# The last two output products of a decoder layer: one order of rows for both column halves, weights split on chip, the residual put into the accumulator banks, and the normalisation on one engine

## The chip, the cores and the metric

One core of a Trainium2 chip. The metric is the device time of one execution in microseconds, the median of several runs; three runs of the kernel before gave 1638.19, 1639.03 and 1640.66. Times in the traces are counted in microseconds from the start of the span of one profiled execution. The engines are TensorE (PE in the profile; PEld is its weight load), VectorE (DVE), ScalarE (ACT), GpSimd (POOL) and SyncE (SP), whose queue issues all the DMAs spoken of here.

## The reference, cut to what matters

```python
# x: 1024 x 2048 float32; proj = x @ w_in, then attention, short convolution and pooling give y
y = jnp.concatenate([y_att, y_conv, y_pool], axis=-1)        # 1024 x 2048
y = jnp.einsum('bse,ed->bsd', y, w_out[l])                   # 2048 x 2048 weights
x = layer_norm(DEEPNORM_ALPHA * x + y, ln_g[l], ln_b[l])     # alpha = 2 ** 0.25

def layer_norm(x, g, b):
    mu = jnp.mean(x32, axis=-1, keepdims=True)
    var = jnp.mean(jnp.square(x32 - mu), axis=-1, keepdims=True)
    return (x32 - mu) * lax.rsqrt(var + LN_EPS) * g + b
```

## The kernel before

Both large products are computed by a scheme of seven half-size products in place of eight. Each float32 operand is split into a high and a low part (`split`, lines 120 to 122: ScalarE casts the high part, VectorE subtracts to get the low one), and each product of two 128-row blocks is three matmuls into one accumulator bank (`mm3`, lines 127 to 130: high x high, high x low, low x high). A bank is 128 x 512 float32; there are eight, four tagged `acc` and four tagged `aux`.

The change is in the output projection. Its seven products are named y11, ys3, ys2, ys1, y22, y12 and ys4, each done for the two column halves i = 0 and 1 of the result, in that order (`sequence`). `out_product` takes one product for one half: for each of eight blocks k it fetches a split weight block (`next_w`, from a running plan of loads) and multiplies it with four row tiles st, into four banks. At the last k the banks are emptied by `evac`. The result has four quarters of rows and columns per half: c11, c12 (rows 0 to 511) and c21, c22 (rows 512 to 1023). y22 completes c21, y12 completes c11, ys4 completes c12; c22 is complete before. `preset_at` puts alpha * x into a bank before the product starts, on ScalarE (line 1065), so that matmuls add to it; the finished bank is added to the tile in SBUF on VectorE (line 1092), and `stats_of` takes the statistics of that piece (line 1024).

Side work (loads, splits, presets, normalisation) is put into slots by `at` and taken out by `tick` after every third triple of matmuls; a scheduler then sets the order on each engine. Loads of weights and of y share four buffers tagged `wr`, so a load waits until the split of the block four loads back is done; stores of the result stand on the same SP queue.

The last product, ys4 for i = 1, is written by hand. Its eight weight blocks are kept whole (`keep_w`: load, then split into `wlast`), and it goes row by row: row tile st takes all eight k into one bank, the bank is added to c12 (line 1227), its statistics are taken, and the row is normalised at once. The last row is done in two half-width parts, so it has two banks of 256 columns.

`norm_steps` normalises one row tile of 128 rows. `stats` combines the statistics and does five small instructions and a square root on ScalarE (line 1128). Each of four pieces of 512 columns then takes a first step (subtract the mean, multiply with g, line 1150) and a second step (multiply with the inverse deviation, add b, line 1151), both on VectorE, and is stored (line 1152). In the tail, that is for the rows 0 to 3 which come last, two of four pieces (one in the last row) go another way:

```python
if tail and c in ((1, 2) if s < 3 else (2,)):
    nc.scalar.activation(r, r, AF.Identity, bias=nt[:, 3:4], scale=nt[:, 2:3])
    nc.gpsimd.tensor_tensor(r, r, g, ALU.mult)
    nc.gpsimd.tensor_tensor(r, r, b, ALU.add)
```

That is one instruction on ScalarE (line 1146) and two on GpSimd (lines 1147 and 1148). Rows 4 to 7 (c21, c22) are normalised earlier, beside y12, on VectorE alone.

Of the kernel before, what the change touches and what calls it, by code (L numbers as in the profile page):

```python
# [36 lines left out]
ALU = mybir.AluOpType  # L37
# [36 lines left out]
def layer(ctx: ExitStack, tc: tile.TileContext, xt, x, wp, wf, b_f, conv_w, pool_w, pool_scale,  # L74
# [903 lines left out]
    for name in WEIGHTS:  # L978
        for i in range(2):
            if (name, i) != ("ys4", 1):  # L980
                plan.extend(WEIGHTS[name](i, k) for k in range(KH))
# [68 lines left out]
    out_banks, last_x = {}, [None]  # L1050

    def preset_at(slot, name, i, st, tag):
# [67 lines left out]
    def norm_steps(s, tail=False):  # L1120
        env = {}

        def stats():
# [10 lines left out]
            if tail:  # L1134
                nc.vector.tensor_scalar(nt[:, 3:4], mv[:, 0:1], nt[:, 2:3], -1.0, ALU.mult, ALU.mult)
            env["mv"], env["nt"] = mv, nt

        def piece(c):
            def go():
# [15 lines left out]
        return [stats] + [piece(c) for c in ((2, 1, 0, 3) if tail else range(4))]  # L1155

    last = {}

    def keep_w(k, slot):
        def load():  # L1160
            last[k] = half("wl", "wr")
            nc.sync.dma_start(last[k], WEIGHTS["ys4"](1, k))

        def parts():
            t = hl("wlast", "xb")
            split_tile(t, last[k])
            last[k] = t

        at(slot, load)
        at(slot + 2, parts)  # L1170

    def after(name, i):
# [20 lines left out]
        if name == "y22":  # L1193
# [4 lines left out]
            else:  # L1198
# [3 lines left out]
                for k in range(KH):  # L1202
                    keep_w(k, 2 + 5 * k // 2)
# [3 lines left out]
    for n, (name, i) in enumerate(sequence[:-1]):  # L1207
        out_product(name, i, tag_of(n))
        after(name, i)
        if n + 2 < len(sequence) and (sequence[n + 2] == ("ys2", 1) or sequence[n + 2][0] in GOES_TO):  # L1210
            for st in range(4):
                preset_at(2 + st, *sequence[n + 2], st, tag_of(n + 2))
    for st in range(4):
        cuts = [0, H] if st < 3 else [0, H // 2, H]
        sl = slice(st * P, st * P + P)
        for n, (c0, c1) in enumerate(zip(cuts, cuts[1:])):
            acc = out_banks["ys4", 1, st]
            if n:
                acc = bank("acc")
                nc.scalar.activation(acc[:, c0:], last_x[0][:, c0:], AF.Copy, scale=ALPHA)  # L1220
            for k in range(KH):
                yt, w = xs["ys4", k], last[k]
                mm3(acc[:, c0:c1], yt[:, 0, sl], yt[:, 1, sl], w[:, 0, c0:c1], w[:, 1, c0:c1], False, k == KH - 1,
                    skip_group_check=True)
# [4 lines left out]
        while side:  # L1229
            for step in side.popleft():  # L1230
                step()
        for step in norm_steps(st, True):
            step()
# [43 lines left out]
```

## Time and profile before

| | |
|---|---|
| median of three runs | 1639.03 us (1638.19 to 1640.66) |
| the profiled execution | 1636.92 us, its span 1635.2 us |
| TensorE | 1553.2 us busy, 6836 instructions |
| VectorE | 1132.4 us busy, 1651 instructions |
| ScalarE | 702.0 us busy, 1254 instructions |
| GpSimd | 400.0 us busy, 317 instructions |
| DMA | 339.92 MB, mean 208 GB/s |

The span runs from the first to the last recorded event of the profiled execution; 1.7 us lie around it. Busy time counts an engine's instructions without its waits. Matmuls overlap, so the start of one and of the next tell more than their durations. In a timeline row, "x4" merges neighbours of the same kind, and the bracket gives the idle time just before and what ended it.

### The profile page before, as it was taken

How to read it: one execution, taken by the hardware profiler on the slowest of the kernel's cores; microseconds unless marked ns; L12 is line 12 of the kernel's file. 1: busy time of each engine (PE TensorE's matmuls, PEld its weight loads, DVE VectorE, ACT ScalarE, POOL GpSimd, SP SyncE). 2: the span in 40 equal slices, each digit the busy share in tenths (PEclk: the TensorE clock that was granted, in tenths of full speed). 3: DMA queues.
4: the chain of work that ended last, by engine and by line, in shares of the span. 5: the costliest groups of instructions: out<-in, count | busy, mean ns of one | idle time of the engine just before them, and what ended most of it. 6: DMA issues, size and time to landing. Idle time of an engine off the chain costs nothing. (4 is left out here: it accounts for less than half of the span.)

```text
span 1635.2 us, 20207 instructions
## 1 busy us (share of the span) xinstructions
PE 1553.2 (95%) x6836; PEld 1254.1 (77%) x6836; DVE 1132.4 (69%) x1651; ACT 702.0 (43%) x1254; POOL 400.0 (24%) x317
## 2 busy tenths in 40 slices
PE   8999999999999999999999999999988998999985
PEld 6887878877788777788877777868776776888765
DVE  6754666666666656478787868586779874567878
ACT  4421221112112225566665656575666554344431
POOL 0132232222222220012222323252326231100005
PEclk9999999999999999999999999999999999999998
DMA  8756988887878667534545454536344437557552
GB/s 248 261 206 208 323 286 291 302 293 257 301 254 306 237 241 247 216 133 160 181 159 177 149 193 149 181 116 210 124 166 142 160 118 251 174 186 231 183 191 103
DMA packets 156807, 339.92 MB, mean 208 GB/s; under 512 B 17952, under 2 KB 27040, under 8 KB 156704
## 3 DMA queue, kind: packets, MB, share of 16 engines
q1 hardware_dynamic: 156704, 338.64, 60.6%
q8 instruction: 53, 0.87, 0.2%
q14 instruction: 50, 0.41, 0.1%
HBM read 247.28 MB, written 91.29 MB: 207 GB/s over the span
## 5 line engine op out<-in xcount | busy, mean ns | idle before, releaser
L122 DVE TENSOR_TENSOR wh<-wr,wh 128x512 fp32r<-128x512 f32 x272 | 204.0, 755 | 97.7 <-ACT wh L121 97.3
L121 ACT CAST wop<-wb 128x1024 fp32r<-128x1024 f32 x76 | 80.0, 1053 | 322.9 <-PE acc L129 142.5
L121 ACT CAST wh<-wr 128x512 fp32r<-128x512 f32 x272 | 166.4, 618 | 94.2 <-DMA wr<-w_out 29.1
L128 PE MATMUL acc<-x,wh 128*128 128x512 f32 x448 | 178.7, 399 | 2.1 <-ACT wh L121 2.1
L130 PE MATMUL aux<-xs,wop 128*128 128x512 f32 x448 | 175.5, 392 | 5.4 <-DVE wop L122 5.2
L130 PE MATMUL acc<-x,wh 128*128 128x512 f32 x448 | 178.3, 398 | 2.3 <-DVE wh L122 2.2
L129 PE MATMUL acc<-x,wh 128*128 128x512 f32 x448 | 176.8, 395 | 0.0
L128 PE MATMUL aux<-xs,wop 128*128 128x512 f32 x448 | 174.6, 390 | 0.0
L129 PE MATMUL aux<-xs,wop 128*128 128x512 f32 x448 | 174.4, 389 | 0.0
L122 DVE TENSOR_TENSOR wop<-wb,wop 128x1024 fp32r<-128x1024 f32 x76 | 107.0, 1408 | 28.2 <-ACT wop L121 28.1
L130 PEld LDWEIGHTS acc<-x,wh 128*128 128x128 f32 x448 | 85.2, 190 | 27.0 <-DVE wh L122 8.9
L130 PEld LDWEIGHTS aux<-xs,wop 128*128 128x128 f32 x448 | 84.1, 188 | 27.3 <-DVE wop L122 9.6
L128 PEld LDWEIGHTS acc<-x,wh 128*128 128x128 f32 x448 | 85.1, 190 | 21.0 <-ACT wh L121 5.4
L129 PEld LDWEIGHTS aux<-xs,wop 128*128 128x128 f32 x448 | 84.1, 188 | 17.6
L128 PEld LDWEIGHTS aux<-xs,wop 128*128 128x128 f32 x448 | 84.1, 188 | 17.4
L129 PEld LDWEIGHTS acc<-x,wh 128*128 128x128 f32 x448 | 85.2, 190 | 15.7
L130 PE MATMUL acc<-xs,wh 128*128 128x512 f32 x224 | 87.7, 392 | 3.0 <-DVE wh L122 3.0
L130 PE MATMUL acc<-xs,wop 128*128 128x512 f32 x224 | 88.0, 393 | 2.7 <-DVE wop L122 2.5
L122 DVE TENSOR_TENSOR pt<-t,pt 128x512 fp32r<-128x512 f32 (+1 forms) x96 | 84.5, 894 | 6.5 <-ACT pt L121 6.3
L128 PE MATMUL acc<-xs,wh 128*128 128x512 f32 x224 | 88.3, 394 | 0.0
L129 PE MATMUL acc<-xs,wh 128*128 128x512 f32 x224 | 87.3, 390 | 0.0
L128 PE MATMUL acc<-xs,wop 128*128 128x512 f32 x224 | 87.2, 389 | 0.0
(266 smaller groups left out, 3628.3 us busy)
## 6 DMA issues: line engine op xcount, KB each, us to landing
wb<-wp SPq DMA_DIRECT2D x116, 512.0 KB, 5.6
wr<-wp SPq DMA_DIRECT2D x112, 256.0 KB, 2.9
wo<-w_out SPq DMA_DIRECT2D x64, 256.0 KB, 5.9
o_dram<-wo SPq DMA_DIRECT2D x64, 256.0 KB, 4.6
wr<-o_dram SPq DMA_DIRECT2D x64, 256.0 KB, 2.9
t_dram<-wb SPq DMA_DIRECT2D x28, 512.0 KB, 6.2
a_dram<-ca SPq DMA_DIRECT2D x28, 512.0 KB, 3.8
b_dram<-cb SPq DMA_DIRECT2D x28, 512.0 KB, 4.7
```

What stands on the lines that cost most here:

```text
L121: nc.scalar.copy(hi, src)
L122: nc.vector.tensor_tensor(lo, src, hi.bitcast(F32), ALU.subtract)
L128: nc.tensor.matmul(acc, wh, xh, start=start, stop=False, **more)
L129: nc.tensor.matmul(acc, wh, xl, start=False, stop=False, **more)
L130: nc.tensor.matmul(acc, wl, xh, start=False, stop=stop, **more)
```

## The change

The last two products, ys4 for both halves, are now both written by hand (`last_product`), and all sixteen weight blocks are loaded and split outside the running plan (`load_last`, `split_last`). The right half's blocks go where they went; the left half's go into the buffers of y12, and their loads are placed beside the first of the four parts below. The order is: rows 0 and 1 of the right half, rows 0 and 1 of the left half, then row 2 of both halves, then row 3 of both halves. The last row is no longer cut in two.

The preset of a ys4 bank is now alpha * x + c12 in one VectorE instruction. So the finished bank holds the finished piece: it isn't added to c12, its statistics are taken from the bank, and the first step of the normalisation reads the bank and writes SBUF. In the tail ScalarE and GpSimd get no pieces any more; all sixteen take their two steps on VectorE.

```diff
             if name == "ys2":
                 nc.scalar.copy(acc, view("c11", i, st))
+            elif name == "ys4":
+                nc.vector.scalar_tensor_tensor(acc, env["x"], ALPHA, view("c12", i, st), ALU.mult, ALU.add)
             else:
                 nc.scalar.activation(acc, env["x"], AF.Copy, scale=ALPHA)
-                last_x[0] = env["x"]
...
-                if tail and c in ((1, 2) if s < 3 else (2,)):
-
-                    nc.scalar.activation(r, r, AF.Identity, bias=nt[:, 3:4], scale=nt[:, 2:3])
-                    nc.gpsimd.tensor_tensor(r, r, g, ALU.mult)
-                    nc.gpsimd.tensor_tensor(r, r, b, ALU.add)
-                else:
-                    nc.vector.scalar_tensor_tensor(r, r, mv[:, 0:1], g, ALU.subtract, ALU.mult)
-                    nc.vector.scalar_tensor_tensor(r, r, nt[:, 2:3], b, ALU.mult, ALU.add)
+                src = out_banks["ys4", c // 2, s] if s < 4 and c % 2 else r
+                nc.vector.scalar_tensor_tensor(r, src, mv[:, 0:1], g, ALU.subtract, ALU.mult)
+                nc.vector.scalar_tensor_tensor(r, r, nt[:, 2:3], b, ALU.mult, ALU.add)
                 nc.sync.dma_start(out[s * P : s * P + P, c * H : c * H + H], r)
...
+    def load_last(i, k):
+        arriving[i, k] = half("wl", "wr")
+        nc.sync.dma_start(arriving[i, k], WEIGHTS["ys4"](i, k))
+
+    def split_last(i, k):
+        last[i, k] = hl("wlast", "xb" if i else "pc" if k < 4 else "qk")
+        split_tile(last[i, k], arriving.pop((i, k)))
...
-    for st in range(4):
-        cuts = [0, H] if st < 3 else [0, H // 2, H]
...
-            r = view("c12", 1, st)[:, c0:c1]
-            nc.vector.tensor_tensor(r, acc[:, c0:c1], r, ALU.add)
-            stats_of(st, r)
...
+    def last_product(i, rows, between=None):
+        for k in range(KH):
+            for st in rows:
+                sl = slice(st * P, st * P + P)
+                yt, w = xs["ys4", k], last[i, k]
+                mm3(out_banks["ys4", i, st], yt[:, 0, sl], yt[:, 1, sl], w[:, 0], w[:, 1], False, k == KH - 1,
                     skip_group_check=True)
                 tick()
+            if between:
+                between(k)
+        for st in rows:
+            stats_of(st, out_banks["ys4", i, st])
+
+    def arrive(k):
+        split_last(0, k)
+        if k + 4 < KH:
+            load_last(0, k + 4)
+
+    for k in range(4):
+        load_last(0, k)
+    last_product(1, (0, 1), arrive)
+    last_product(0, (0, 1))
...
+    for st in range(2):
+        for step in norm_steps(st):
+            step()
+    for st in range(2, 4):
+        for i in range(2):
+            last_product(i, (st,))
+        for step in norm_steps(st):
             step()
```

The orders on the engines are the scheduler's. TensorE's agrees up to the place shown first. That is TensorE in the product y12 for i = 1, at weight block k = 6 (`wh_13052`): the four banks `acc` are its four row tiles, line 128 is the part that needs the block's high half, lines 129 and 130 those after it. Before:

```order
L128 MATMUL acc_12871<-wh_13052,xy_2227_12500 128x512
L128 MATMUL acc_12897<-wh_13052,xy_2227_12500 128x512
L128 MATMUL acc_12916<-wh_13052,xy_2227_12500 128x512
L129 MATMUL acc_12842<-wh_13052,xy_2227_12500 128x512
L130 MATMUL acc_12842<-wh_13052,xy_2227_12500 128x512
L129 MATMUL acc_12871<-wh_13052,xy_2227_12500 128x512
```

and now (`aux_13107` is the bank of row 0, right half, of ys4; `wlast` its weight blocks, `xys` its y blocks):

```order
L130 MATMUL aux_13107<-wlast_12933,xys_2256_12667 128x512
L128 MATMUL aux_13107<-wlast_12989,xys_2264_12708 128x512
L129 MATMUL aux_13107<-wlast_12989,xys_2264_12708 128x512
L130 MATMUL aux_13107<-wlast_12989,xys_2264_12708 128x512
L128 MATMUL aux_13107<-wlast_13042,xys_2280_12791 128x512
L129 MATMUL acc_12842<-wh_13052,xy_2227_12500 128x512
L130 MATMUL acc_12842<-wh_13052,xy_2227_12500 128x512
L129 MATMUL acc_12871<-wh_13052,xy_2227_12500 128x512
```

Thirteen matmuls of ys4 (blocks 0 to 3 whole, and one matmul of block 4) have moved in between the high-half and the low-half matmuls of that weight block. A little later, where y12 ends, TensorE before went on to the left half of ys4 with its first block `wh_13113`:

```order
L130 MATMUL acc_12897<-wh_13074,xy_2232_12538 128x512
L129 MATMUL acc_12916<-wh_13074,xy_2232_12538 128x512
L130 MATMUL acc_12916<-wh_13074,xy_2232_12538 128x512
L128 MATMUL aux_13093<-wh_13113,xys_2241_12596 128x512
L128 MATMUL aux_13111<-wh_13113,xys_2241_12596 128x512
L128 MATMUL aux_13130<-wh_13113,xys_2241_12596 128x512
```

and now goes on in the right half, rows 0 and 1 (`aux_13107`, `aux_13140`), with block 5 (`wlast_13086`) and then block 6 (`wlast_13135`):

```order
L130 MATMUL acc_12897<-wh_13072,xy_2232_12538 128x512
L129 MATMUL acc_12916<-wh_13072,xy_2232_12538 128x512
L130 MATMUL acc_12916<-wh_13072,xy_2232_12538 128x512
L129 MATMUL aux_13107<-wlast_13086,xys_2288_12834 128x512
L130 MATMUL aux_13107<-wlast_13086,xys_2288_12834 128x512
L129 MATMUL aux_13140<-wlast_13086,xys_2288_12834 128x512
L130 MATMUL aux_13140<-wlast_13086,xys_2288_12834 128x512
L128 MATMUL aux_13107<-wlast_13135,xys_2300_12887 128x512
L129 MATMUL aux_13107<-wlast_13135,xys_2300_12887 128x512
```

The first matmul of the left half has moved from the 21st place after the common part (`wh_13113` above) to the 69th. VectorE near the end (`c_1909`, `c_2085`, `c_1964`, `c_2117` hold the four pieces of rows 2 and 3; `mv` and `nt` are mean and scale, `bst` the statistics; lines 1150 and 1151 of before are 1144 and 1145 now). Before:

```order
L1129 RECIPROCAL mv_13458<-mv_13458 128x1
L1227 TENSOR_TENSOR c_2117_11953<-acc_13507,c_2117_11953 128x256
L1132 TENSOR_SCALAR nt_13462<-mv_13458,nt_13462 128x1
L1024 BN_STATS bst_12968<-c_2117_11953 128x6
L1133 TENSOR_SCALAR nt_13462<-nt_13462,mv_13458 128x1
L1126 BN_AGGR mv_13535<-bst_12968 128x2
L1135 TENSOR_SCALAR nt_13462<-mv_13458,nt_13462 128x1
L1151 SCALAR_TENSOR_TENSOR c_1909_10844<-c_1909_10844,nt_13462,gb_12715 128x512
L1151 SCALAR_TENSOR_TENSOR c_2117_11953<-c_2117_11953,nt_13462,gb_12717 128x512
L1131 TENSOR_SCALAR nt_13539<-mv_13535 128x1
L1150 SCALAR_TENSOR_TENSOR c_2085_11772<-c_2085_11772,mv_13535,gb_12711 128x512
L1150 SCALAR_TENSOR_TENSOR c_1909_10844<-c_1909_10844,mv_13535,gb_12711 128x512
```

and now:

```order
L1144 SCALAR_TENSOR_TENSOR c_2117_11953<-acc_13289,mv_13420,gb_12713 128x512
L1024 BN_STATS bst_12968<-acc_13300 128x6
L1133 TENSOR_SCALAR nt_13424<-mv_13420,nt_13424 128x1
L1024 BN_STATS bst_12968<-acc_13311 128x6
L1134 TENSOR_SCALAR nt_13424<-nt_13424,mv_13420 128x1
L1127 BN_AGGR mv_13490<-bst_12968 128x2
L1145 SCALAR_TENSOR_TENSOR c_1909_10844<-c_1909_10844,nt_13424,gb_12715 128x512
L1145 SCALAR_TENSOR_TENSOR c_2085_11772<-c_2085_11772,nt_13424,gb_12715 128x512
L1145 SCALAR_TENSOR_TENSOR c_1964_11125<-c_1964_11125,nt_13424,gb_12717 128x512
L1145 SCALAR_TENSOR_TENSOR c_2117_11953<-c_2117_11953,nt_13424,gb_12717 128x512
L1132 TENSOR_SCALAR nt_13494<-mv_13490 128x1
L1144 SCALAR_TENSOR_TENSOR c_1909_10844<-c_1909_10844,mv_13490,gb_12711 128x512
```

The additions of line 1227 are gone, the statistics read the banks `acc`, and four pieces stand in a row where three did.

## Rows read from the trace of the kernel before

**Rows 1.** The page, part 1: busy time, share of the span and instructions of each engine.

```profile
PE 1553.2 (95%) x6836; PEld 1254.1 (77%) x6836; DVE 1132.4 (69%) x1651; ACT 702.0 (43%) x1254; POOL 400.0 (24%) x317
```

**Rows 2.** Windows of the last 75 us: busy time and instructions per engine, granted clock, DMA.

```profile
core 0: us, PE busy (x) PEld busy (x) DVE busy (x) ACT busy (x) POOL busy (x), PEclk, DMA share, GB/s
1560.00:1580.00 20.00, 18.03 (x77) 14.21 (x76) 18.27 (x32) 7.30 (x13) 0.00 (x0) 0.98 0.76 241
...
1600.00:1620.00 20.00, 18.04 (x103) 15.73 (x101) 19.55 (x41) 4.32 (x8) 12.31 (x8) 1.00 0.24 90
1620.00:1636.00 16.00, 0.00 (x0) 0.00 (x0) 10.59 (x16) 2.52 (x4) 9.77 (x7) 0.57 0.41 149
```

**Rows 3.** Timeline of TensorE, the two waits: start, duration, engine, line, out<-in [idle before <-releaser].

```profile
1566.05 1.07 PE L128 MATMUL acc<-wh,xy 128*128 128x512 f32 x4
1567.55 0.50 PE L129 MATMUL acc<-wh,xy 128*128 128x512 f32 x1 [0.43 <-DVE wh L122]
...
1573.91 1.20 PE L128 MATMUL aux<-wh,xys 128*128 128x512 f32 x4 [1.53 <-ACT wh L121]
```

**Rows 4.** Timeline of VectorE, SP's queue and ScalarE: what stands behind the two waits.

```profile
1566.81 0.69 DVE L122 TENSOR_TENSOR wh<-wr,wh 128x512 fp32r<-128x512 f32 x1
...
1567.53 0.94 SPq L187 DMA_DIRECT2D wr<-w_out  x2
...
1573.24 1.32 ACT L121 CAST wh<-wr 128x512 fp32r<-128x512 f32 x2 [7.85 <-DMA wr<-w_out]
```

**Rows 5.** Timeline of TensorE, the last product, with the first and last half-width matmul.

```profile
1580.40 0.39 PE L128 MATMUL acc<-wlast,xys 128*128 128x512 f32 x1
...
1598.98 0.39 PE L130 MATMUL acc<-wlast,xys 128*128 128x512 f32 x1
...
1612.13 0.28 PE L128 MATMUL acc<-wlast,xys 128*128 128x256 f32 x1
...
1617.76 0.28 PE L130 MATMUL acc<-wlast,xys 128*128 128x256 f32 x1
```

**Rows 6.** VectorE's groups by form, 1596 to 1636: busy us, mean ns | idle before.

```profile
L1150 DVE SCALAR_TENSOR_TENSOR c<-c,mv,gb 128x512 f32<-128x512 f32 x9 | 11.9, 1367 | 0.0
L1151 DVE SCALAR_TENSOR_TENSOR c<-c,nt,gb 128x512 f32<-128x512 f32 x9 | 7.6, 886 | 0.0
L1024 DVE BATCH_NORM_STATS2 bst<-c 128x6 f32<-128x512 f32 x7 | 4.7, 687 | 0.1
...
L1132 DVE TENSOR_SCALAR nt<-mv,nt 128x1 f32<-128x1 f32 x4 | 1.1, 270 | 0.1
L1133 DVE TENSOR_SCALAR nt<-nt,mv 128x1 f32<-128x1 f32 x4 | 0.8, 210 | 0.1
...
L1126 DVE BATCH_NORM_AGGREGATE mv<-bst 128x2 f32<-128x24 f32 x3 | 0.8, 261 | 0.1
```

**Rows 7.** Timeline of VectorE and GpSimd after the last matmul.

```profile
1620.29 1.41 DVE L1151 SCALAR_TENSOR_TENSOR c<-c,nt,gb 128x512 f32<-128x512 f32 x2
...
1621.48 3.00 POOL L1147 TENSOR_TENSOR c<-c,gb 128x512 f32<-128x512 f32 x2 [1.29 <-ACT c L1146]
...
1621.67 5.03 DVE L1150 SCALAR_TENSOR_TENSOR c<-c,mv,gb 128x512 f32<-128x512 f32 x3
...
1630.23 1.59 POOL L1148 TENSOR_TENSOR c<-c,gb 128x512 f32<-128x512 f32 x1
```

**Rows 8.** VectorE's groups by form, 1540 to 1575, columns as in rows 6.

```profile
L1151 DVE SCALAR_TENSOR_TENSOR c<-c,nt,gb 128x512 f32<-128x512 f32 x16 | 11.0, 745 | 0.0
L1150 DVE SCALAR_TENSOR_TENSOR c<-c,mv,gb 128x512 f32<-128x512 f32 x9 | 6.7, 740 | 0.0
```

**Rows 9.** VectorE's groups by form, whole program: a step from a bank, and the residual step.

```profile
L725 DVE SCALAR_TENSOR_TENSOR m<-aux,ncum,m 128x512 f32<-128x512 f32 x16 | 11.9, 745 | 7.6 <-ACT t L700 7.2
...
L1043 DVE SCALAR_TENSOR_TENSOR c<-xr,c 128x512 f32<-128x512 f32 x8 | 5.5, 682 | 0.0
```

**Rows 10.** The stores of line 1152: time from issue to landing.

```profile
DMA to landing us min/median/max: 2.3/2.7/5.9
```

More of the change, by code (lines that the diff above doesn't have):

```diff
@@ L979, in layer @@
         for i in range(2):
-            if (name, i) != ("ys4", 1):
+            if name != "ys4":
                 plan.extend(WEIGHTS[name](i, k) for k in range(KH))
@@ L1049, in layer @@
     GOES_TO = {"y22": "c21", "y12": "c11", "ys4": "c12"}
-    out_banks, last_x = {}, [None]
+    out_banks = {}
     def preset_at(slot, name, i, st, tag):
@@ L1118, in load_gb, with norm_steps @@
                 gb.append(t)
-    def norm_steps(s, tail=False):
+    def norm_steps(s):
         env = {}
@@ L1143, in go @@
                 g, b = gb[c // 2][:, cs], gb[2 + c // 2][:, cs]
-                if tail and c in ((1, 2) if s < 3 else (2,)):
-                    nc.scalar.activation(r, r, AF.Identity, bias=nt[:, 3:4], scale=nt[:, 2:3])
-                    nc.gpsimd.tensor_tensor(r, r, g, ALU.mult)
-                    nc.gpsimd.tensor_tensor(r, r, b, ALU.add)
-                else:
-                    nc.vector.scalar_tensor_tensor(r, r, mv[:, 0:1], g, ALU.subtract, ALU.mult)
-                    nc.vector.scalar_tensor_tensor(r, r, nt[:, 2:3], b, ALU.mult, ALU.add)
+                src = out_banks["ys4", c // 2, s] if s < 4 and c % 2 else r
+                nc.vector.scalar_tensor_tensor(r, src, mv[:, 0:1], g, ALU.subtract, ALU.mult)
+                nc.vector.scalar_tensor_tensor(r, r, nt[:, 2:3], b, ALU.mult, ALU.add)
                 nc.sync.dma_start(out[s * P : s * P + P, c * H : c * H + H], r)
             return go
[L1155 to L1170, printed above, removed]
+        return [stats] + [piece(c) for c in range(4)]
+    last, arriving = {}, {}
+    def load_last(i, k):
[4 more added lines that the diff above has]
+        split_tile(last[i, k], arriving.pop((i, k)))
     def after(name, i):
@@ L1202, in after @@
                 for k in range(KH):
-                    keep_w(k, 2 + 5 * k // 2)
+                    at(2 + 5 * k // 2, lambda k=k: load_last(1, k))
+                    at(4 + 5 * k // 2, lambda k=k: split_last(1, k))
     sequence = [(name, i) for name in WEIGHTS for i in range(2)]
     tag_of = lambda n: "acc" if n < 4 or n % 2 else "aux"
-    for n, (name, i) in enumerate(sequence[:-1]):
+    for n, (name, i) in enumerate(sequence[:-2]):
         out_product(name, i, tag_of(n))
         after(name, i)
-        if n + 2 < len(sequence) and (sequence[n + 2] == ("ys2", 1) or sequence[n + 2][0] in GOES_TO):
+        name, i = sequence[n + 2]
+        if (name, i) == ("ys2", 1) or name in ("y22", "y12"):
@@ L1211, in layer @@
             for st in range(4):
-                preset_at(2 + st, *sequence[n + 2], st, tag_of(n + 2))
-    for st in range(4):
-        cuts = [0, H] if st < 3 else [0, H // 2, H]
[L1215 to L1223, printed above, removed]
+                preset_at(2 + st, name, i, st, tag_of(n + 2))
+        elif name == "ys4":
+            for m in range(4):
+                preset_at(2 + m, "ys4", m % 2, 2 * i + m // 2, tag_of(n + 2))
@@ L1229, in layer @@
[L1229 to L1232, printed above, removed]
+            if between:
[10 more added lines that the diff above has]
+    last_product(0, (0, 1))
+    while side:
+        for step in side.popleft():
+            step()
@@ L1233, in layer @@
+    for st in range(2):
+        for step in norm_steps(st):
+            step()
+    for st in range(2, 4):
+        for i in range(2):
+            last_product(i, (st,))
+        for step in norm_steps(st):
             step()
```

2 lines of the change are left out of this document (removed).

## Prediction

> **What bounds the kernel now.** I read four views in this order: the page's first part, the windows of the last stretch, the timeline of single engines there, and the groups by form. Over the program TensorE is busy 95% of the span [rows 1], so on the whole it sets the time. The change touches only the last 75 us, and that stretch must be read by itself. Three things are to be seen there [rows 2]. From 1560 to 1580 TensorE is busy 18.03 of 20 us while VectorE is busy 18.27 and GpSimd does nothing. From 1600 to 1620 VectorE is busy 19.55 of 20, now with GpSimd beside it. From 1620 to 1636 TensorE has nothing left, and the kernel only normalises and stores. So there are two losses: TensorE waits twice before 1580, and 17 us pass after its last matmul.
>
> The two waits [rows 3]: at 1567.55 for the low half of a weight block, which VectorE began to split at 1566.81, and at 1573.91 for the high half of the next product's first block, which ScalarE cast at 1573.24 because its load was issued at 1567.53 and took 5.7 us [rows 4]. Between waits a 512-column matmul starts every 0.2266 us: 82 of them lie between 1580.40 and 1598.98; the 48 half-width ones at the end start every 0.1198 us, from 1612.13 to 1617.76 [rows 5].
>
> The tail is read from the forms [rows 6]. The two normalising steps take 1367 and 886 ns there. The timeline says why [rows 7]: at 1620.29, with GpSimd idle, two take 1.41 us; at 1621.67, under GpSimd's work from 1621.48 on, three take 5.03. In the earlier stretch, where GpSimd does nothing, the same two lines take 740 and 745 ns [rows 8]. An instruction starts some 0.08 us before the end of the one ahead (two of 0.745 in 1.41), so a step costs 0.665 in a full queue and a statistic 0.61 (687 ns less 0.08).
>
> **The change, part by part.** I count from 1566.05, the last point to which TensorE's queue is the same in both (its four high-half matmuls on weight block 6 of y12).
>
> *TensorE.* From there 240 matmuls stood in the queue before, 192 wide and 48 half-wide: 192 x 0.2266 + 48 x 0.1198 = 49.26 us, so without waits the last would have been over at 1615.31. It was over at 1617.76 + 0.12 = 1617.88: 2.57 us are waits and restarts. Now 216 wide ones remain, 216 x 0.2266 = 48.95 us. The split of the last row into halves goes, which gains 48 x 0.1198 - 24 x 0.2266 = 0.31. If both waits go, the last matmul starts at 1614.77 and ends, by its 0.39 us [rows 5], at 1615.16: **2.9 us** earlier.
>
> Do they go? At the first, 13 matmuls of the last product now stand in front of the low half, so it is needed at 1566.05 + 17 x 0.2266 = 1569.90. VectorE's queue ahead of that split holds one step-size instruction more than before (three bank presets in, a first and a second step out), so the split starts at 1566.81 + 0.67 and is done at about 1568.2. At the second, TensorE no longer turns to a fresh block: it finishes rows 0 and 1 of the right half, whose blocks 0 to 5 are loaded. Block 6 is the next that must arrive. Its load stands on SP behind three stores and waits for the buffer that the split above frees: issue 1568.3, 5.7 us, cast and split 1.3: 1575.3, needed after 60 matmuls at 1579.65. Behind it VectorE's queue holds block 7, four second steps, eight splits for the left half, four additions to c11, four bank presets and six statistics before the left half's block 7 is split: 0.6 + 4 x 0.665 + 8 x 0.6 + 4 x 0.6 + 4 x 0.665 + 6 x 0.61 = 16.8, so 1592.1, needed at 1566.05 + 132 x 0.2266 = 1595.96. The eight new loads share four buffers with the old ones; each is issued when a split four back is done, and at 5.7 us they stay ahead of that queue. Slack everywhere: 1.7 us at least, some 3.5 on the left half.
>
> *The presets.* Eight bank presets move from ScalarE to VectorE and take the residual and C12 in one. VectorE writing to a bank has no row here. Nearest is its residual step with the same operands into SBUF, 682 ns [rows 9]; the far end is 1367 ns [rows 6]; the cheapest full-width instruction costs 0.61 in a queue, so nothing can be gained by it. I take 0.665, as rows 9 are nearest. At the far end 8 x 0.7 = 5.6 us would use up the slack of 3.5 and cost 2.1. ScalarE loses its presets there; it sat idle for 7.85 us beforehand, waiting for a load [rows 4], so this gains nothing.
>
> *Tail on VectorE.* Gone are the nine additions of banks to C12 (two of half width); the first step and the statistics read the bank directly. Added are the pieces that ScalarE and GpSimd had (seven of sixteen), 14 steps. VectorE's queue can start the last part when TensorE has finished both left-half banks of rows 0 and 1, the 138th matmul from 1566.05: 1566.05 + 137 x 0.2266 + 0.39 = 1597.48. From there it holds 5 statistics (3.05), 32 steps (21.28) and 20 small ones of 0.21 to 0.27 [rows 6], at 0.15 in a queue (3.04): 1624.85, the end of the last 0.08 later. The same end counted from the last matmul at 1615.16: one statistic, six small ones and 12 steps, 0.61 + 0.91 + 7.98 = 1624.66. The two chains meet within 0.2 us, so VectorE hardly waits for the last row and whatever delays TensorE delays the end one for one.
>
> A bank as a step's source has a row: 745 ns [rows 9], no more than from SBUF. A bank as the source of a statistic has none; between 0.61 and a step's 0.665 I take 0.61. The Trainium skill (Perfetto Trace Analysis, Optimizing Scalar/DVE Operations) gives VectorE about 60 ns of access per instruction on SBUF and 125 on PSUM; its 65 ns on 13 instructions would make the estimate 0.85 us longer, and the row for the step does not bear it out.
>
> *The stores.* Before, GpSimd's last piece ends at 1630.23 + 1.59 = 1631.82, and the span 3.38 us later. Now the last four pieces end 0.665 apart, each followed by a store that takes 2.3 to 2.7 us to land [rows 10]; I add 0.3 of that 0.4 for four close together. The span ends at 1624.93 + 3.38 + 0.3 = 1628.6.
>
> **Sum:** 2.9 from TensorE and 3.7 from the tail (17.16 us after the last matmul before, 13.44 now), 6.6 us of a span of 1635.2. The profiled execution would take 1636.92 - 6.6 = 1630.3. The runs' median is 1639.03, 2.1 above that execution; there I forecast **1632.4 us**. About 0.2%, 3.3 us, is what a measurement of this kernel tells from no change.
>
> **The rivals.**
> *A. The weights come late.* All sixteen blocks of the last two products go through four buffers on one queue, with stores in front. For it: the wait at 1573.91 is of this kind, and a late split holds up the additions, presets and statistics behind it on VectorE. Against: 3.5 us of slack. Two turns of the four buffers feed the left half; at 9.5 us a load instead of 5.7 they lose 7.6, of which 4 pass the slack: 1636.4, no difference that can be told. Smaller delays leave 1633 to 1635.
> *B. A bank is the dearer place.* If what VectorE reads from a bank costs as much more as a step with 745 ns costs against one with 682 [rows 9], then 13 x 0.063 = 0.8 us: 1633.2.
> *C. VectorE alone is slower than three engines.* If the long steps of the tail are long by themselves and not by GpSimd, the 32 steps take the tail's mean of 1.13 us, 1.05 in a queue: 32 x 0.38 = 12.3 us more, 1644.7, slower. It decides from 0.87 us a step on, where the 6.6 are used up. Against it stands the pair at 1620.29 in 1.41 us, in the same tail with GpSimd idle [rows 7]. The Trainium skill (same page and section) advises taking work off a full VectorE, which speaks for this rival, and adds that GpSimd shares a read port with it so that this may not help; rows 7 show the second.
> *D. The tail does not shrink.* The order does what it says for TensorE, but the steps of the last rows bunch behind the last matmul and only its 2.9 us are gained: 1636.1. Against: the two chains above.
>
> **How the numbers follow.** Forecast 0.70, A 0.13 (a third of it still faster by over 0.2%), B 0.08, C 0.05, D 0.04. Faster: 0.70 + 0.04 + 0.08 = 0.82; within 0.2%: 0.09 + 0.04 = 0.13; slower: 0.05. The forecast's own range is 1630 to 1634. The low end takes the 0.3 of the stores and the 0.8 and 1.6 us by which the shown runs scatter about their median: 1629.8. The high end takes in A and D: 1636.5.
>
> **What would show it.** Right: no TensorE wait after 1566; steps of some 0.74 us in the tail; GpSimd empty there; last matmul near 1615, last step near 1625, span near 1628.6. Wrong: a TensorE wait for a `wlast` block (A); tail steps over 0.87 us (C); statistics from a bank well over 0.69 us (B); VectorE idle after the last matmul (D).

## The result and the profile after

Four runs of the changed kernel gave a median of **1628.70 us** (1623.25 to 1629.93); the kernel before, run beside it, 1638.65 (1638.19 to 1640.66, four runs). The ratio is **0.9937, 95% interval 0.9913 to 0.9961**: faster, by 9.95 us of the medians. The forecast was 1632.4, with a range from 1629.8: the side was right, the time lies 1.1 us below the range. The profiled execution took 1629.22 us, its span 1627.5; forecast for it was 1630.3.

The page's busy line of the changed kernel answers to [rows 1], the windows of its last stretch to [rows 2]:

```profile
PE 1553.6 (95%) x6812; PEld 1254.3 (77%) x6812; DVE 1129.3 (69%) x1659; ACT 691.9 (43%) x1238; POOL 381.5 (23%) x303
```

```profile
1560.00:1580.00 20.00, 20.00 (x90) 16.54 (x89) 18.87 (x32) 6.08 (x10) 0.00 (x0) 1.00 0.76 250
1600.00:1620.00 20.00, 14.27 (x63) 11.47 (x62) 19.78 (x45) 0.88 (x3) 0.00 (x0) 0.94 0.44 157
1620.00:1636.00 16.00, 0.00 (x0) 0.00 (x0) 3.79 (x7) 0.00 (x0) 0.00 (x0) 0.70 0.18 66
```

From 1560 to 1580 TensorE now has no gap (18.03 us before), GpSimd does nothing in the tail, and VectorE is through before 1624. TensorE's timeline of the changed kernel answers to [rows 3, 5]:

```profile
1550.98 1.07 PE L128 MATMUL acc<-wh,xy 128*128 128x512 f32 x4
...
1556.15 0.73 PE L129 MATMUL acc<-wh,xy 128*128 128x512 f32 x1 [4.11 <-DVE wh L122]
...
1565.15 1.07 PE L128 MATMUL acc<-wh,xy 128*128 128x512 f32 x4
...
1613.88 0.39 PE L130 MATMUL acc<-wlast,xys 128*128 128x512 f32 x1
```

1565.15 is the point from which the prediction counted (1566.05 before); call it Q. Both waits behind it are gone. The row at 1550.98 is the same step three weight blocks earlier, four high-half matmuls on block 3; call it P. The wait behind P stands in both kernels; before:

```profile
1551.88 1.07 PE L128 MATMUL acc<-wh,xy 128*128 128x512 f32 x4
1557.05 0.53 PE L129 MATMUL acc<-wh,xy 128*128 128x512 f32 x1 [4.10 <-DVE wh L122]
```

It will matter, and it costs more than its 4.11 us. These are the changed kernel's windows over the wait and just behind it:

```profile
1551.00:1556.10 5.10, 1.05 (x5) 0.55 (x3) 5.10 (x10) 1.25 (x3) 0.00 (x0) 1.00 0.95 298
1556.10:1559.60 3.50, 3.45 (x8) 2.74 (x9) 3.50 (x9) 0.09 (x1) 0.00 (x0) 0.52 0.69 209
```

VectorE, which has to split the low half of block 3, is busy without a gap all through the wait. Behind it the granted clock is 0.52, near the lower of its two levels, 1.2 and 2.4 GHz, and eight matmuls take 3.52 us from the first to what follows them, where eight at 0.2266 take 1.81: 1.7 us more. VectorE's timeline at the end, with the start of the tail, the wait for the last matmul and the last step, answers to [rows 7]:

```profile
1595.94 1.38 DVE L1024 BATCH_NORM_STATS2 bst<-aux 128x6 f32<-128x512 f32 x2 [6.62 <-PE aux L130]
...
1614.30 0.70 DVE L1024 BATCH_NORM_STATS2 bst<-acc 128x6 f32<-128x512 f32 x1 [0.22 <-PE acc L130]
...
1621.12 2.74 DVE L1145 SCALAR_TENSOR_TENSOR c<-c,nt,gb 128x512 f32<-128x512 f32 x4
```

And its groups by form from 1596 to 1636 answer to [rows 6]:

```profile
L1145 DVE SCALAR_TENSOR_TENSOR c<-c,nt,gb 128x512 f32<-128x512 f32 x16 | 10.9, 743 | 0.0
L1144 DVE SCALAR_TENSOR_TENSOR c<-c,mv,gb 128x512 f32<-128x512 f32 x8 | 5.9, 741 | 0.0
L1144 DVE SCALAR_TENSOR_TENSOR c<-aux,mv,gb 128x512 f32<-128x512 f32 x4 | 3.0, 744 | 0.0
L1144 DVE SCALAR_TENSOR_TENSOR c<-acc,mv,gb 128x512 f32<-128x512 f32 x4 | 3.0, 740 | 0.0
L1024 DVE BATCH_NORM_STATS2 bst<-acc 128x6 f32<-128x512 f32 x4 | 2.8, 688 | 0.2 <-PE acc L130 0.2
L1024 DVE BATCH_NORM_STATS2 bst<-aux 128x6 f32<-128x512 f32 x2 | 1.4, 698 | 6.6 <-PE aux L130 6.6
```

All 32 steps take 0.74 us, from a bank (`aux`, `acc`) or from SBUF (`c`); the long steps of 1367 and 886 ns are gone. The eight presets, by their line: duration in ns (minimum, median, maximum) and start of the first and last:

```profile
L1065 DVE SCALAR_TENSOR_TENSOR aux<-xr,c x4: 687/698/699, 1559.9 to 1568.3; 128x512 f32<-128x512 f32 x4
L1065 DVE SCALAR_TENSOR_TENSOR acc<-xr,c x4: 677/677/678, 1581.5 to 1587.5; 128x512 f32<-128x512 f32 x4
```

Counted from Q the forecast holds: the last matmul ends 49.12 us after it (forecast 49.11), the last step 58.71 (58.88), the span 62.35 (62.55). So three things stood open: why the medians differ by 9.95 and not by 6.8; which of the three edits gains; and whether the wait behind P can go.

### The profile page after: what moved, and what is told of

It is laid out like the page before. It is cut to its first block, busy times and chain, and to the rows that moved or that the text cites. A ratio compares the mean times of both kernels' runs of the same rounds, so it can differ in the third digit from the quotient of the medians.

```text
span 1627.5 us, 20130 instructions
## 1 busy us (share of the span) xinstructions
PE 1553.6 (95%) x6812; PEld 1254.3 (77%) x6812; DVE 1129.3 (69%) x1659; ACT 691.9 (43%) x1238; POOL 381.5 (23%) x303
## 5 line engine op out<-in xcount | busy, mean ns | idle before, releaser
L122 DVE TENSOR_TENSOR wh<-wr,wh 128x512 fp32r<-128x512 f32 x264 | 199.4, 761 | 92.4 <-ACT wh L121 91.8
L121 ACT CAST wh<-wr 128x512 fp32r<-128x512 f32 x264 | 161.5, 618 | 83.6 <-PE acc L130 27.9
L122 DVE TENSOR_TENSOR wop<-wb,wop 128x1024 fp32r<-128x1024 f32 x76 | 102.7, 1352 | 27.1 <-ACT wop L121 27.0
```

The lines of the kernel that those rows point to most:

```text
L121: nc.scalar.copy(hi, src)
L122: nc.vector.tensor_tensor(lo, src, hi.bitcast(F32), ALU.subtract)
```

## The experiments

For each profile two stretches are given, from P and from Q to the end of the span. The kernel before has 83.32 and 69.15 us (1635.2 less 1551.88 and 1566.05), the changed kernel 76.52 and 62.35. Theory 1 says that the change is worth this difference, 6.8, and that the rest is scatter between executions. Theory 2 says that the unchanged part before P also became faster.

### Both kernels again

No edit.

> The kernel before, once more, for the scatter of its executions. Theory 1 (the change is worth some 6.8 us, all after the last common point, and the rest of the 10 us between the medians is scatter of the unchanged part): executions between 1636 and 1641 us, this profile's common point (the four L128 matmuls on weight block 6 of y12) anywhere within about 1.5 us of 1566.05, and from it to the end of the span again 69.2 us, within 0.4. Theory 2 (the unchanged part itself became some 3 us faster): the common point stays within 0.4 us of 1566.05 and the executions sit at 1638 to 1641.

> The changed kernel, once more. Theory 1: from the common point (1565.15 in its first profile) to the end of the span again 62.4 us, within 0.4, so 6.8 less than in the kernel before; the common point itself moves by up to 1.5 us from profile to profile and overlaps with that of the kernel before; the median of five rounds lies 6 to 8 us under that of the kernel before, not 10. Theory 2: the common point is again 1 us or more ahead of that of the kernel before, and the medians again differ by 9 to 11 us.

TensorE's timeline of the kernel before, repeated (span 1642.9): P and Q.

```profile
1559.47 1.07 PE L128 MATMUL acc<-wh,xy 128*128 128x512 f32 x4
...
1574.70 1.07 PE L128 MATMUL acc<-wh,xy 128*128 128x512 f32 x4
```

The same of the changed kernel, repeated (span 1637.7):

```profile
1561.21 1.07 PE L128 MATMUL acc<-wh,xy 128*128 128x512 f32 x4
...
1575.38 1.07 PE L128 MATMUL acc<-wh,xy 128*128 128x512 f32 x4
```

Before: 83.43 and 68.20. Changed: 76.49 and 62.32. The stretch from P repeats within 0.1 us, and P is now later in the changed kernel, by 1.7 us. The stretch from Q doesn't repeat in the kernel before (68.20, expected 69.2 within 0.4): the first of its two waits behind Q is missing this time, and the way from P to Q is 1.06 us longer instead. So P is the better point to count from. Medians 1644.33 and 1637.53; against 33 executions of the kernel before (median 1644.74) the changed kernel has 0.9957 (0.9940 to 0.9974), 7.2 us. That is theory 1. Its figures for single executions were too tight: Q moved by 8.65 us in the kernel before and 10.23 in the changed one, not 1.5, and the 33 executions of the kernel before went from 1637.95 to 1652.88 with a standard deviation of 3.6 us, not from 1636 to 1641.

A third and a fourth time, beside later experiments:

> The changed kernel, a third time, as the measure for the other three: 76.5 us from the four high-half matmuls on block 3 to the end of the span, 62.3 from those on block 6, and a median 6 to 8 us under the kernel before.

> The changed kernel beside it on the same chip, and more executions of both kernels. Theory 1 (the change is worth 6.9 us, and what the medians show beyond is scatter): 76.5 us from block 3 to the end for the fourth time, and a median 6 to 8 us under the kernel before. Theory 2 (a part before that point also became some 3 us faster): 76.5 as well, but a median 9 to 11 us under it.

From P 76.50 and 77.22 (the second missed by 0.7; from Q it has 62.38). Ratios 0.9944 (0.9926 to 0.9962) and 0.9961 (0.9938 to 0.9985), medians 9.9 and 5.0 us under the kernel before, neither within the 6 to 8 expected. The four comparisons thus give 9.95, 7.2, 9.9 and 5.0 us; the traces 6.8 and 6.9 in the first two pairs, 6.1 with the longest of the four stretches. Theory 2 wanted 9 to 11 each time, and an earlier P; in all the profiles of this study P lies between 1551 and 1561.4, in kernels with the old last stretch as in those with the new. It falls, though a rest of about 1 us (the mean of the four is 8.0) can't be told from scatter.

### VectorE alone, in the kernel before

```diff
-                if tail and c in ((1, 2) if s < 3 else (2,)):
+                if tail and c in ():
```

> The kernel before with only the normalising pieces of the last four rows moved to VectorE; order and additions stay. Theory 1 (GpSimd's work in the tail costs VectorE about what it saves it): VectorE gets 14 more steps, 14 x 0.665 = 9.3 us, and its 18 steps fall from 1367 and 886 ns to 745, 6.9 us; the 1.1 us that GpSimd's last piece trails are saved: 1 us slower, from 1 us faster to 3 slower, steps of 0.74 us. Rival (VectorE alone is where the tail's gain comes from): 3 to 4 us faster than the kernel before. Second rival (the long steps are long by themselves): steps stay near 1.1 us and it is 10 us or more slower.

Ratio to the kernel before 1.0000 (0.9979 to 1.0021); 83.92 and 69.96 us. VectorE's groups by form in its tail:

```profile
L1150 DVE SCALAR_TENSOR_TENSOR c<-c,mv,gb 128x512 f32<-128x512 f32 x16 | 11.0, 746 | 0.0
L1151 DVE SCALAR_TENSOR_TENSOR c<-c,nt,gb 128x512 f32<-128x512 f32 x16 | 10.9, 746 | 0.0
```

Steps of 1367 and 886 ns fall to 746 when GpSimd is idle, and 14 more of them eat that up. Theory 1 holds: alone this edit gains nothing.

### Three engines, in the changed kernel

```diff
...
+                if tail and c in ((1, 2) if s < 3 else (2,)):
+                    nc.scalar.activation(r, src, AF.Identity, bias=nt[:, 3:4], scale=nt[:, 2:3])
+                    nc.gpsimd.tensor_tensor(r, r, g, ALU.mult)
+                    nc.gpsimd.tensor_tensor(r, r, b, ALU.add)
+                else:
...
```

> The changed kernel with the pieces that ScalarE and GpSimd had before given back to them; order, weights and C12 in the banks stay. Theory 1 (sharing gains nothing): VectorE loses 14 steps of 0.665 us (9.3 us) but its other 18 slow to 0.9 to 1.4 us (6.9 us), and GpSimd's four-operation pieces end last by up to 1 us: within 2 us of the changed kernel on either side. Rival (VectorE alone is the gain): 3 us or more slower than the changed kernel. Second rival (VectorE is the bound in the tail and three engines are better): 3 us or more faster, span about 1624.

76.61 and 62.65 us; median 1638.45, 0.9 above the changed kernel's beside it. So in the new order too, VectorE alone is worth 0.3 us at most.

### Work on GpSimd beside it

```diff
...
+                nc.gpsimd.tensor_copy(scratch[0][:, :2], mv[:, 0:2])
+                for _ in range(beside):
+                    nc.gpsimd.tensor_tensor(scratch[0], scratch[0], gb[0][:, :H], ALU.mult)
...
```

`beside` is 4 for each of the last four rows. The copy of two columns makes the work wait for the row's mean.

> The changed kernel with work beside it that is part of no output: four multiplications of 128x512 on GpSimd for each of the last four rows. Theory 1 (GpSimd's work stretches VectorE's steps on two tensors): the 14 GpSimd instructions of the kernel before cost 18 VectorE steps 6.9 us, 0.49 each, so 16 cost some 8: steps of 1.1 to 1.5 us on average in the tail, 68 to 74 us from the common point to the end of the span; statistics, which read one tensor, stay at 0.69. Rival (the long steps in the kernel before are long by themselves, or by ScalarE): steps stay at 0.74, 62.3 us.

88.79 and 74.02 us. From Q that is 11.7 more than without, 0.73 for each of 16 multiplications, where theory 1 had some 8; the ratio to the kernel before is 1.0034 (1.0016 to 1.0051). VectorE's groups by form in the tail, to be read against those of the changed kernel above:

```profile
L1154 DVE SCALAR_TENSOR_TENSOR c<-c,nt,gb 128x512 f32<-128x512 f32 x16 | 20.1, 1312 | 0.0
L1153 DVE SCALAR_TENSOR_TENSOR c<-c,mv,gb 128x512 f32<-128x512 f32 x8 | 8.6, 1080 | 0.0
L1153 DVE SCALAR_TENSOR_TENSOR c<-aux,mv,gb 128x512 f32<-128x512 f32 x4 | 3.0, 738 | 0.0
L1153 DVE SCALAR_TENSOR_TENSOR c<-acc,mv,gb 128x512 f32<-128x512 f32 x4 | 2.9, 735 | 0.0
L1024 DVE BATCH_NORM_STATS2 bst<-acc 128x6 f32<-128x512 f32 x4 | 2.7, 679 | 0.0
```

The steps with both tensors in SBUF go from 743 and 741 to 1312 and 1080 ns; those that read a bank, and the statistics, do not get longer. Only GpSimd was given work here, so its work alone makes such steps long; and without it they are short in the kernel before too (746 ns, above). So GpSimd is the cause of the long steps in [rows 6].

### The old order, with the other two edits

The left half goes through `out_product` again, its weights split as they arrive, and the right half row by row; the presets are placed in the order of the halves, and the last row stays in one piece:

```diff
...
-    for n, (name, i) in enumerate(sequence[:-2]):
+    for n, (name, i) in enumerate(sequence[:-1]):
...
-    last_product(1, (0, 1), arrive)
-    last_product(0, (0, 1))
...
+    for st in range(4):
+        last_product(1, (st,))
...
```

> The changed kernel with the old order alone: the left half of ys4 k by k over four rows with its weights split as they arrive, then the right half row by row. C12 in the banks and VectorE alone stay. Counted from the common point to the end of the span, where the changed kernel takes 62.3 us and the kernel before 68.2 to 69.2. Theory 1 (order and additions each carry about half of the gain): TensorE's waits at the end of y12 and at the first left-half block return (1.3 to 2.1 us) and, since all left banks become complete together and rows then come every 5.4 us to a VectorE that needs 7.3, 12 us pass after the last matmul and not 9.6: 66 to 67.5. Rival (the order is worth its TensorE time only): 64 to 64.5. Second rival (the order is not what gains): within 0.5 us of 62.3.

82.86 and **68.92 us**: nearly all of the gain is gone, more than theory 1 had. The ratio to the kernel before is 0.9986 (0.9970 to 1.0003). TensorE's timeline: after Q at 1571.88 both waits are back, and the last matmul.

```profile
1574.05 0.50 PE L129 MATMUL acc<-wh,xy 128*128 128x512 f32 x1 [1.10 <-DVE wh L122]
...
1578.99 1.42 PE L128 MATMUL aux<-wh,xys 128*128 128x512 f32 x4 [1.88 <-ACT wh L121]
...
1625.84 0.39 PE L130 MATMUL acc<-wlast,xys 128*128 128x512 f32 x1
```

VectorE's timeline, the start of the tail and its end:

```profile
1606.10 2.74 DVE L1024 BATCH_NORM_STATS2 bst<-aux 128x6 f32<-128x512 f32 x4 [10.62 <-PE aux L130]
1609.95 0.70 DVE L1024 BATCH_NORM_STATS2 bst<-acc 128x6 f32<-128x512 f32 x1 [1.12 <-PE acc L130]
...
1634.43 2.74 DVE L1147 SCALAR_TENSOR_TENSOR c<-c,nt,gb 128x512 f32<-128x512 f32 x4
```

The last matmul starts 53.96 us after Q instead of 48.73. VectorE gets its first complete row at 1609.95, 38.1 us after Q (30.8 in the changed kernel), and has 27.2 us of work from there without a gap. So the order is worth 6.4 us from P (6.6 from Q), of 6.9.

Against the kernel before with VectorE alone (83.92), this run differs by C12 in the banks and by the last row, which is done in one piece; together they gain only 1.06 us. The tail from the last matmul's start to the last step's end did become shorter, 11.33 us for 14.54; but TensorE came 2.05 us later (53.96 for 51.91). The windows from 1580 to 1590 show where, of this run and then of that one:

```profile
1580.00:1590.00 10.00, 10.00 (x38) 8.07 (x38) 9.85 (x16) 3.35 (x7) 0.00 (x0) 0.84 0.80 269
```

```profile
1580.00:1590.00 10.00, 10.00 (x45) 8.24 (x45) 9.44 (x16) 6.25 (x11) 0.00 (x0) 1.00 0.73 237
```

The two waits behind Q add up to 3.0 us, for 2.1. After them TensorE has a granted clock of 0.84 and does 38 matmuls instead of 45; VectorE, with the presets, is busy 9.85 of 10 us.

### The additions back

ScalarE presets a bank, VectorE adds it to C12, and statistics and first steps read the sum in SBUF:

```diff
-            elif name == "ys4":
-                nc.vector.scalar_tensor_tensor(acc, env["x"], ALPHA, view("c12", i, st), ALU.mult, ALU.add)
             else:
                 nc.scalar.activation(acc, env["x"], AF.Copy, scale=ALPHA)
...
+            r = view("c12", i, st)
+            nc.vector.tensor_tensor(r, out_banks["ys4", i, st], r, ALU.add)
+            stats_of(st, r)
```

> The changed kernel with the eight additions of C12 back: ScalarE presets alpha * x, VectorE adds C12 to the bank into SBUF, and statistics and steps read SBUF. Order and VectorE alone stay. Theory 1: six of the eight additions lie in VectorE's full queue of the tail, 6 x 0.6 = 3.6 us, so 65.9 us from the common point to the end of the span (62.3 in the changed kernel), with statistics and first steps as long as from a bank (0.69 and 0.74 us). Rival (a bank is dearer to read than SBUF, so that the additions buy something back): statistics and first steps shorter by 0.06 us or more and the gap under 3 us. Second rival (VectorE only waits for TensorE there): within 0.5 us of 62.3.

> The run with the eight additions back, once more, beside the changed kernel on the same chip. If its gain is real: 74.4 us again, within 0.4, between the same two points, and a median some 2 us under the changed kernel's. If it was scatter of executions: 76.5, and medians within 1 us.

All three theories of the first run missed: it is *shorter*, 74.41 us from P. The second time it is 75.02, outside the 0.4 allowed: a wait of 0.61 us for a late weight block came in. (Q is no common point here, since TensorE's order differs from P on.) TensorE's timeline of the first run, P and what now stands behind it:

```profile
1559.19 1.07 PE L128 MATMUL acc<-wh,xy 128*128 128x512 f32 x4
1560.53 0.50 PE L128 MATMUL aux<-wlast,xys 128*128 128x512 f32 x1 [0.27 <-ACT aux L1065]
...
1564.34 0.50 PE L129 MATMUL acc<-wh,xy 128*128 128x512 f32 x1 [1.25 <-DVE wh L122]
...
1618.50 0.39 PE L130 MATMUL acc<-wlast,xys 128*128 128x512 f32 x1
```

ScalarE had presets ready in time, and ten matmuls of the last product stand where TensorE waited 4.11 us. What is left there are waits of 0.27 and 1.25 us, and the granted clock behind them, from 1564.3 to 1568, is 1.00. The last matmul starts 59.3 us after P, 62.9 in the changed kernel. The tail behind it is longer by the additions: 11.1 us to the last step's end where the changed kernel has 9.6. VectorE's groups by form in the tail, from 1597 to 1634:

```profile
L1142 DVE SCALAR_TENSOR_TENSOR c<-c,mv,gb 128x512 f32<-128x512 f32 x16 | 11.1, 743 | 0.0
...
L1024 DVE BATCH_NORM_STATS2 bst<-c 128x6 f32<-128x512 f32 x6 | 4.0, 679 | 0.0
```

First steps and statistics from SBUF take 743 and 679 ns, from a bank 740 to 744 and 688 to 698, so a bank is hardly dearer. The gain of 1.5 to 2.1 us is shown by the traces; the medians could not show it: 1633.69 the second time, beside 1633.49 for the changed kernel (six executions each).

This run also tells what the order is worth when the additions stay. The kernel before with VectorE alone has the additions too, and took 83.92 us from P; the new order (with the last row in one piece) takes 8.9 to 9.5 us off that, more than the whole change gained.

### Rows 0 and 1 of the left half one behind the other

```diff
-    last_product(0, (0, 1))
+    last_product(0, (0,))
+    last_product(0, (1,))
```

> The changed kernel with the left halves of rows 0 and 1 as two products one behind the other, so that row 0 is complete some 5 matmuls (1.1 us) sooner. Theory 1 (the two chains of the prediction meet: VectorE waited 0.22 us for the last matmul, and what stands behind that statistic in its queue stays the same): the start of the tail moves 1.1 us ahead, the wait for the last matmul grows by as much, and the end stays: 62.1 to 62.6 us from the common point. Rival (VectorE's backlog alone sets the end): 61.2 us.

76.60 and 62.41 us. VectorE starts 0.4 us sooner, where 1.1 was expected, and the wait for the last matmul grows by as much, from 0.22 to 0.59; the end stays. That is theory 1: TensorE's last matmul sets it.

### Towards a faster version

Only the right-half banks of rows 0 and 1 keep ScalarE's preset and the later addition:

```diff
-            elif name == "ys4":
+            elif name == "ys4" and not (i == 1 and st < 2):
...
+            if i == 1 and st < 2:
+                r = view("c12", i, st)
+                nc.vector.tensor_tensor(r, out_banks["ys4", i, st], r, ALU.add)
...
```

> A mixture, for a version faster than both. The run with the additions back ended sooner than the changed kernel (74.4 us against 76.5 from the four high-half matmuls on weight block 3 of y12's right half to the end of the span): with ScalarE's presets the scheduler had banks ready in time to put 25 matmuls of the last product into TensorE's 4.1 us wait at that block. Here only the two right-half banks of rows 0 and 1 keep ScalarE's preset and the addition, where VectorE has idle time later; the other six take C12 on VectorE. Theory 1 (the early preset fills the wait, the additions cost VectorE's tail): the wait stays under 2 us as there, and the tail after the last matmul falls from 11 to some 9.7 us: 72.5 to 73.3. Rival (the six presets back on VectorE delay the splits again): a wait of 3 to 4 us, 75 to 76.5.

> The mixture with the left halves of rows 0 and 1 as two products, one behind the other. If VectorE's start in the tail now sets the end, row 0 ready 0.4 to 1.1 us sooner gives as much: 72 to 73. If TensorE's last matmul sets it, no difference from the mixture within 0.3 us.

77.89 us from P, worse than either theory, and 78.05 with the two products apart: no difference, so TensorE's last matmul sets the end here too. The ratios to the kernel before are 0.9973 (0.9957 to 0.9989) and 0.9960 (0.9944 to 0.9976). ScalarE's timeline in the mixture, and behind it TensorE's, show why:

```profile
1565.49 1.20 ACT L121 CAST wh<-wr 128x512 fp32r<-128x512 f32 x2 [4.50 <-DMA wr<-w_out]
1566.60 1.11 ACT L1067 ACTIVATE aux<-xr 128x512 f32<-128x512 f32 x2
```

```profile
1567.25 0.79 PE L128 MATMUL aux<-wlast,xys 128*128 128x512 f32 x1 [4.77 <-ACT aux L1067]
```

ScalarE sat idle for 4.50 us ahead of a cast whose weights landed late, with the preset behind it in its queue; the preset's x had landed 17 us before P, and the first two of the four `aux` banks were free from 1562.2 on. The gap was 4.77 us, not 4.11, and the tail after it 10.6 us, not 9.7. The next kernel changes only the order in which each group of four presets is placed:

```diff
-                preset_at(2 + m, "ys4", m % 2, 2 * i + m // 2, tag_of(n + 2))
+                preset_at(2 + m, "ys4", 1 - m // 2, 2 * i + m % 2, tag_of(n + 2))
```

> The mixture again, with the order of the four early presets changed: first the two right-half banks of rows 0 and 1 (ScalarE), then the left-half ones (VectorE). In the first mixture ScalarE's preset stood behind the cast of a weight block that landed 4.5 us later, and TensorE waited 4.77 us for it; now it stands ahead of that cast, as in the run with the additions back, and 12 to 25 matmuls of the last product are ready when TensorE needs work. Theory 1 (the place of the preset in ScalarE's queue decides the wait; the additions decide the tail): a wait under 2 us, 72.3 to 73.5 us from the four high-half matmuls on block 3 to the end of the span, against 76.5 in the changed kernel and 74.4 to 75.0 with the additions back. Rival (the wait is VectorE's lateness, whoever presets): a wait of 3 us or more, 75.5 or more.

**73.72 us** from P. ScalarE's timeline, the preset now ahead of that cast, and TensorE's with P, the wait that is left and the end:

```profile
1555.19 1.20 ACT L1067 ACTIVATE aux<-xr 128x512 f32<-128x512 f32 x2 [0.52 <-DVE c L1093]
1559.74 1.28 ACT L121 CAST wh<-wr 128x512 fp32r<-128x512 f32 x2 [3.35 <-DMA wr<-w_out]
```

```profile
1555.08 1.07 PE L128 MATMUL acc<-wh,xy 128*128 128x512 f32 x4
...
1566.15 0.50 PE L128 MATMUL aux<-wlast,xys 128*128 128x512 f32 x1 [1.83 <-ACT wlast L121]
...
1614.13 0.39 PE L130 MATMUL acc<-wlast,xys 128*128 128x512 f32 x1
```

Theory 1 holds for the wait: at block 3 it is gone; a smaller one, for a late weight block, stands 11 us on. The time is 0.2 us over its 72.3 to 73.5. Two things came with the new order: the presets stand ahead of the cast, and the two right-half ones get the banks that come free first, so that 20 matmuls of both rows stand behind P and not ten of row 0. The run with the additions back had the old order of presets, and its first preset for the right half stood ahead of the cast: 0.27 us of wait for it there, 4.77 in the first mixture. So the place ahead of the cast lets TensorE start; what the second bank adds was not measured by itself. From P this kernel is 2.8 us shorter than the changed one and 9.6 shorter than the kernel before. Its ratio to the latter is 0.9950 (0.9931 to 0.9968), median 1634.88, beside 1638.66 for the changed kernel with 0.9961: the intervals overlap, so that it beats the changed kernel is shown by the traces (one of this kernel, four of the other) and not by the times. From the run with the additions back it differs by 0.7 to 1.3 us from P, little more than the 0.7 by which one kernel's stretch was seen to move.

## Why the prediction was right, and where it was wrong

*TensorE, 2.9 us: right against the trace that it was read from.* Both waits went, the last matmul ended 49.12 us after Q. In the repeated kernel before, with one wait behind Q instead of two, only 1.9 us of this lie behind Q. Rival A, late weights, did not come: no wait behind Q. It is near, though: with the wait behind P filled, TensorE waited 0.61 us (additions back, the second time) and 1.83 us (second mixture) for late blocks.

*The tail, 3.7 us: right in its sum.* From the last matmul's end to the end of the span it took 13.23 us (1627.5 less 1614.27), forecast 13.44. The two chains met as worked out: VectorE waited 0.22 us for the last matmul. That its own chain came out has some luck in it: it began 30.79 us after Q and not 31.43, since row 0's statistic didn't wait for row 1's bank, and held six statistics and not five; the two nearly cancel. Steps cost 0.74, statistics from a bank 688 to 698 ns, so rivals B and C fall, and the stores took 3.64 us after the last step (forecast 3.68). The rows behind C were read rightly: the long steps are GpSimd's doing, as the extra work beside the changed kernel shows.

*Whose gain it is: not asked.* The prediction reckoned the tail's 3.7 us as one sum and did not divide it among the edits. Undone one at a time in the changed kernel, the order is worth 6.4 us, VectorE alone at most 0.3, and C12 in the banks *loses* 1.5 to 2.1: TensorE gives back earlier more than the tail saves. In the old order C12 in the banks gains 1.1 us at most (with the last row in one piece). With the additions left in, the order is worth 8.9 to 9.5.

*The presets: the price was right, the cost at nothing was wrong.* Writing a bank takes VectorE 0.68 to 0.70 us. But the move also fixed when those banks are ready. Left on ScalarE, ahead of the cast, the early ones let TensorE fill the wait behind P, which the prediction took as given; in the mixture's second order this is worth 2.8 us against the changed kernel.

*The step that failed* is the last: "The runs' median is 1639.03, 2.1 above that execution; there I forecast 1632.4", with the low end taken from "the 0.8 and 1.6 us by which the shown runs scatter". (The three terms of the low end give 1629.7, not 1629.8.) The offset of 2.1 us between a profiled execution and the median belongs to no kernel: in the four comparisons the changed kernel's profiled execution stood 0.5 and 1.95 above, 1.4 below and 1.1 above its median. So this term was off by 2.6 of the 3.7 us between forecast and result; 0.9 is the earlier Q, in a part that did not change, and 0.2 the sum itself. Three runs within 2.5 us had suggested a scatter that 33 runs put at a standard deviation of 3.6 and a width of 15; by half of that, 1.8, even a mean of four such runs scatters. The low end should have stood some 2 us lower, and the high end higher as well: the changed kernel's later medians are 1637.53, 1633.49 and 1638.66, and the kernel before's went from 1638.65 in the first comparison to between 1643.41 and 1644.74 in the others. The difference between the kernels was forecast well (6.6 us; 6.1 to 6.9 from P); an absolute median could not be, to a few us.

## What to carry to other kernels

Take an order first from when the consumer gets its first complete piece and from what the producer can do while it waits: here that was worth 6.4 of 6.9 us, and the eight additions saved along the way less than nothing, because the instruction that saved them made banks ready later. An instruction that makes a buffer ready belongs on a queue where nothing late stands in front of it; the order of presets, two of them ahead of or behind a cast, decided 4.2 us (73.72 against 77.89 us). For differences below the scatter of executions, compare the traces from the last common instruction on, and take the range's width from many runs and not from three.

## What the runs showed of the hardware that was not expected

- GpSimd's multiplications slow VectorE's steps on two SBUF tensors from 0.74 to 1.08 and 1.31 us on average, but not those with one operand in a bank (735 to 738 ns), nor statistics, which read one tensor (679 from a bank; 687 from SBUF, [rows 6]). The Trainium skill (SBUF — State Buffer, SBUF: two separate sides) says that the two engines contend for one pair of ports, VectorE in an instruction with two SBUF inputs or in a two-port mode; the rows agree for the first, form by form, and the second was not tried.
- A bank costs VectorE hardly more to read than SBUF: 740 and 744 ns against 741 and 743 for the first step, 688 and 698 against 679 and 687 for a statistic. Nor is it dearer to write: 677 to 699 ns for a preset, 682 for the same operands into SBUF [rows 9]. The Trainium skill (Perfetto Trace Analysis, Optimizing Scalar/DVE Operations) gives about 60 ns of access on SBUF and 125 on PSUM; the 65 ns between them are not there.
- TensorE's granted clock was 0.52 behind the wait of 4.1 us, and 1.00 behind one of 1.25 us (additions back).
- With the same work on TensorE up to P, P came at 1551 to 1561 us in 16 profiles; from P on, three of five repeats agree with the first profile of their kernel within 0.1 us, the other two within 0.7.
